# S5 feedthrough tables on four column tiles, and eleven front matmuls, in an S5/MoBA trunk

## The chip, the cores and the metric

The kernel runs on one core of a Trainium2 chip. The metric is the device time of one execution in microseconds (us). Three executions of the kernel before took 1000.97, 1001.4 and 1001.5 us; the median is 1001.4. In the text PE is TensorE, DVE is VectorE, ACT is ScalarE, POOL is GpSimd and SP is SyncE, which issues most of the transfers.

## What is computed

Two layers on a sequence of 256 tokens of width 1024, batch 1, all in float32. A layer is

```python
h = h + 0.5 * swiglu(rms_norm(h), w_gate, w_up, w_down)
h = h + mixer(rms_norm(h))         # layer 0: S5, layer 1: MoBA attention
h = h + 0.5 * swiglu(rms_norm(h), w_gate, w_up, w_down)
```

The feed-forward parts have an inner width of 2816. The change touches the S5 mixer, a diagonal state-space layer of 64 groups with 16 channels and 64 complex states each:

```python
u = h @ w_in
dt = exp(log_dt); lam = exp((a_re + i a_im) * dt)
coef = (lam - 1) / (a_re + i a_im);  bb = coef * b
state[t] = lam * state[t-1] + bb @ u[t]          # per group
y = Re(c @ state) + d * u
g = gelu(y); g = g * sigmoid(g @ w_glu); out = g @ w_out
```

## The kernel before

**Stages.** `phases` runs in order: f00 (first feed-forward part), S5, f01, f10, MoBA, f11. Every large product is a sum of three: activations and weights are each split into a high part that the matmul takes as float32r and a low remainder, and high x high, high x low and low x high are added (`mm3`, L396). Weights stream through three raw buffers of 1 MB (class `Stream`); `split` (L72) makes the high half on ACT (L84, L90) and the low half on DVE (L85, L91), and `pump` is called at fixed places in the product loops.

**The front.** `busy(7)` (L1376) gives PE seven products of ones; `quarter(0)` transposes the first quarter of x (L1332) into two PSUM tiles and writes the activations' high part on ACT (L1339) and low part on DVE (L1340); `busy(3)` follows; `gu0` (L457) then takes the first feed-forward column block by quarters of the depth (L471), and between its parts come quarters 1 to 3 of x. `quarter` uses the PSUM tiles `A1` and `A3`, of which there is one each, so a quarter's transposes have to wait until the quarter before has been read by L1339 and L1340. The sums of squares (L1354) go to POOL (`factors`, L1356), whose result goes through PE and DVE back to columns (L1365 to L1372).

**The tables.** S5 does not scan over all tokens; it works on pieces of four tokens, and a generator, `tables` (L618), prepares the matrices for that while f00 runs. `fill` (L1316) advances a slot counter by 0.7 or 1.4 at each step of the f00 products and calls the generator once per step; a `yield` hands control back. First come the parameters (L658 to L802): the exponentials on ACT, and sine, cosine, powers and `coef` as a long chain of small POOL instructions (helpers at L686, L690 and L692), with one reciprocal on DVE (L774). Then a loop (L919) runs a list of DVE work, each piece due at a slot and paid from a credit that grows with the slots, and PE work `later`, at slots set by `LAG` and `PACE`. The powers of lambda (`e_init`, `e_step`, L697 to L715) begin with a DVE copy of POOL's result (L701). For each of eight blocks `b` of four pairs of groups, `spread` (L844) lays the block-diagonal factors out, `t1_tab` (L856) transposes and stores the input table `dA`, and `t3_tab` (L872) makes the feedthrough table: the response of output token t to input token s inside a piece of four, with `d` on its diagonal. For a block it is

- eight products, one for each of four pairs and real and imaginary part, 32 rows by 64 columns each, all into PSUM partitions 0 to 31 (L880), and a ninth that adds the diagonal `DG[b]` with the identity (L882);
- eight ACT copies out of PSUM (L886), for each of four input tokens s and two groups g, to partitions 32 s to 32 s + 31, shifted by s and masked by `gm` so that a group does not reach its neighbour;
- one POOL send of 128 x 512 values to `dB[b]` (L888).

`d_diag` (L867) makes the diagonal on POOL. S5 loads `dA`, `dE` and `dB` back (L945 to L955). Its products use halves of the output partitions: L986 alternates between PSUM partitions 0 to 63 and 64 to 127.

```python
for i in range(2):                                              # t1, L982
    for q in range(4):
        c = i * 256 + q * 64
        for r in HALVES:
            mm(ps[r, c:c + 64], tv[:, i, q, r], U[:, 4 * b + q, :, :], start=True, stop=True)   # L986
```

Of the kernel before, what the change touches and what calls it, by code (L numbers as in the profile page):

```python
# [10 lines left out]
F32 = mybir.dt.float32  # L11
F32R = mybir.dt.float32r
AF = mybir.ActivationFunctionType
OP = mybir.AluOpType
AX = mybir.AxisListType
# [103 lines left out]
def trunk_kernel(ctx: ExitStack, tc, x, ffn_norm, ffn_w_gate, ffn_w_up, ffn_w_down, mix_norm,  # L119
# [3 lines left out]
    nc = tc.nc  # L123
# [13 lines left out]
    def psR():  # L137
        return pp.tile([128, 512], F32, name="pR", tag="R", bufs=2)
# [4 lines left out]
    mm = nc.tensor.matmul  # L143
# [6 lines left out]
    dB = [dp.tile([128, 1536], F32, name=f"dB_{b}") for b in range(NB)]  # L150
# [84 lines left out]
    ident = cst[:, 0:128]  # L235
# [7 lines left out]
    h = [h2[:, t, :] for t in range(2)]  # L243
# [22 lines left out]
    if "s5" in phases:  # L266
        rho = cp.tile([128, 32], F32, name="rho")
        tstack, lstack, xstack = ExitStack(), ExitStack(), ExitStack()
        tabp = tstack.enter_context(tc.tile_pool(name="tab", bufs=1))
        scn = tabp.tile([32, 2, 128], F32, name="scn")  # L270
        ldt = tabp.tile([32, 2], F32, name="ldt")
        dnat = tabp.tile([32, 32], F32, name="dnat")
        nc.gpsimd.dma_start(ldt, s5_log_dt[0].rearrange("(q g) -> q g", g=2))
        nc.gpsimd.dma_start(scn[:, 0, :], s5_a_re[0].rearrange("(q g) p -> q (g p)", g=2))
        nc.gpsimd.dma_start(scn[:, 1, :], s5_a_im[0].rearrange("(q g) p -> q (g p)", g=2))
        nc.gpsimd.dma_start(dnat, s5_d[0].rearrange("(q c) -> q c", c=32))
    st = Stream(nc, units, rp, hp)

    gT = cp.tile([128, 48], F32, name="gT")
# [17 lines left out]
    X = {}  # L297
# [320 lines left out]
    def tables(tp):  # L618

        V, P = nc.vector, nc.gpsimd  # L620

        def T(name, *shape):
            return tp.tile([128] + list(shape), F32, name=name)
# [9 lines left out]

        MPs = [T(f"mp{k}", 2, 4, 4, 2, 16) for k in range(2)]
        TT = T("tt", 2, 4, 4, 2, 16)
        t3s = [T(f"t3{k}", 4, 4, 32) for k in range(2)]
        cf7 = T("cf7", 7, 2)
        for k, n in enumerate(range(15, 1, -2)):
            for i in range(2):
                P.memset(cf7[:, k, i:i + 1], (-1.0) ** ((n - i) // 2) / math.factorial(n - i))  # L640
        for m in MPs + [TT] + t3s:
            P.memset(m, 0.0)
        bn = [tp.tile([128, 32, 16], F32, name="bn", tag="n0", bufs=2) for i in range(2)]
        cn = tp.tile([128, 1280], F32, name="cn", tag="n1", bufs=2)[:, 0:1024].rearrange("p (i a c) -> p i a c", i=2, c=64)
# [16 lines left out]
        ps = psR()  # L661
# [2 lines left out]
        nc.tensor.transpose(ps[:, 64:96], dtb.rearrange("q g p -> q (g p)"), ident[0:32, 0:32])  # L664
        prm = T("prm", 3, 32)
        V.tensor_copy(prm.rearrange("p a b -> p (a b)"), ps[:, 0:96])
        gm = tp.tile([32, 2], F32, name="gm")
        i2 = ident[0:32, 0:32].rearrange("p (g n) -> p g n", g=2)
        V.reduce_sum(gm, i2, axis=AX.X)
        i16 = tp.tile([32, 16], F32, name="i16")  # L670
        P.tensor_tensor(i16, i2[:, 0], i2[:, 1], op=OP.add)
        dTq = T("dTq", 32)
        ar, ai, dt = prm[:, 0, :], prm[:, 1, :], prm[:, 2, :]
        are, aim, mag = T("are", 32), T("aim", 32), T("mag", 32)
        tt(are, ar, dt, OP.mult)
# [3 lines left out]
        yield  # L679

        ps = psR()
        nc.tensor.transpose(ps[0:32, 0:32], dnat, ident[0:32, 0:32])
        V.tensor_copy(dTq[0:32, :], ps[0:32, 0:32])

        def pt(o, a, b, op):
            P.tensor_tensor(o, a, b, op=op)  # L686
# [1 line left out]
        def pts(o, a, s1, op0, s2=None, op1=None):  # L688
            if op1 is None:
                P.tensor_scalar(o, a, s1, None, op0=op0)  # L690
            else:
                P.tensor_scalar(o, a, s1, s2, op0=op0, op1=op1)  # L692
# [27 lines left out]
        q, y, y2, e0, e1, den = (T(n, 32) for n in ("q", "y", "y2", "e0", "e1", "den"))  # L720
# [50 lines left out]
            pt(lt[:, 1, :, o], u2[:, 1], w2[:, 0], OP.add)  # L771

        cfr, cfi = T("cfr", 32), T("cfi", 32)
        V.reciprocal(rden, den)  # L774
        pts(y, lr, -1.0, OP.add)
        pt(e0, y, ar, OP.mult)
# [15 lines left out]
        for i, a in enumerate((ltr, lti)):  # L792
            av = a.rearrange("p (b q) s -> p b q s", b=8)
            for k in range(2):
                P.tensor_copy(L[i][:, :, 0, k], av)
                for s in range(3):
                    o = L[i][:, :, 1, k, :, s]
# [46 lines left out]
        def spread(b):  # L844

            d_diag(b)
            tv, mv = (o.rearrange("p i q s g n -> p (i q) s g n") for o in (TT, MPs[b % 2]))
            zv = ZC[b].rearrange("p m i q (s n) -> p m (i q) s n", n=16)
            for g, r in enumerate(HALF):
                nc.scalar.activation(tv[r, :, :, g, :], zv[r, 0, :, 1:5], AF.Copy)  # L850
                nc.scalar.activation(mv[r, :, :, g, :], zv[r, 1, :, 1:5], AF.Copy)
            for i in range(2):
                nc.gpsimd.dma_start(dB[b][:, 512 * i:512 * i + 512].rearrange("p (q x) -> p q x", q=4),
                                    TT[:, i].rearrange("p q t g n -> p q (t g n)"))
# [10 lines left out]
        DG = {}  # L865

        def d_diag(b):  # L867
            DG[b] = tp.tile([32, 4, 16], F32, name="dg", bufs=2)
            P.tensor_tensor(DG[b], i16[:, None, :].to_broadcast([32, 4, 16]),
                            dTq[0:32, 4 * b:4 * b + 4, None].to_broadcast([32, 4, 16]), op=OP.mult)  # L870

        def t3_tab(b):  # L872

            t3 = t3s[b % 2]
            ps = psR()
            zc = ZC.pop(b)
            pk = ps[0:32, 0:256].rearrange("p (q t c) -> p q t c", q=4, c=16)
            for qq in range(4):
                for i in range(2):
                    mm(ps[0:32, qq * 64:(qq + 1) * 64], MPs[b % 2][:, i, qq, 3].rearrange("p g n -> p (g n)"),  # L880
                       zc[:, 0, i, qq, 0:64], start=qq == 0 and i == 0, stop=False, skip_group_check=True)
            mm(pk[:, :, 0, :], ident[0:32, 0:32], DG.pop(b), start=False, stop=True, skip_group_check=True)  # L882
            tv = t3.rearrange("p q t (g c) -> p q t g c", c=16)
            for s in range(4):
                for g in range(2):
                    nc.scalar.activation(tv[32 * s:32 * s + 32, :, s:4, g, :], pk[:, :, 0:4 - s, :], AF.Identity,  # L886
                                         scale=gm[:, g:g + 1])
            nc.gpsimd.dma_start(dB[b][:, 1024:1536], t3.rearrange("p q t c -> p (q t c)"))  # L888

        work = []  # L890

# [10 lines left out]
        def add_spread(b):  # L902
            work.append((0.0, B_AT, (spread, b), [(t3_tab, b), (t1_tab, b, 0), (t1_tab, b, 1)], 3 * (b - 1)))
# [15 lines left out]
        while work or later or dma:  # L919
# [4 lines left out]
            if later and later[0][0] <= now:  # L924
                f = later.pop(0)
                f[1](*f[2:])
                done[0] += 1
            while work and work[0][1] <= now and credit >= work[0][0] and done[0] >= work[0][4]:
                w, _, f, pe, _ = work.pop(0)
                f[0](*f[1:])  # L930
                credit -= w
                t = max([now + LAG] + [a[0] + PACE for a in later])
# [369 lines left out]

    pre = []
    tab = tables(tabp) if "s5" in phases else iter(())
    next(tab, None)
    slot = [0]
# [16 lines left out]
    def quarter(q, mid=lambda: None):  # L1323

        if not X:
            X[phases[0], "x"] = True
            X["h"], X["l"] = home(XP[0], phases[0])
        pv = [psA(1 + 2 * k)[:, 0:256] for k in range(2)]
        for k in range(2):
            for t in range(2):  # L1330
                c = (2 * q + k) * 128
                nc.tensor.transpose(pv[k][:, t * 128:(t + 1) * 128].rearrange("p (s i) -> p i s", s=4),  # L1332
                                    xn[t][:, c:c + 128], ident)
            if k == 0:
                mid()
        for k in range(2):
            g = gT[:, 2 * q + k:2 * q + k + 1]
            xh, xl = (X[p][:, 2 * q + k, :] for p in "hl")
            nc.scalar.activation(xh, pv[k], AF.Identity, scale=g)  # L1339
            nc.vector.scalar_tensor_tensor(xl, pv[k], g, xh.bitcast(F32), op0=OP.mult, op1=OP.subtract)  # L1340

    def busy(n):

        ps = psR()
        for _ in range(n):
            mm(ps[:, 0:128], ones, ones, start=True, stop=True)
# [29 lines left out]
    busy(7)  # L1376
    quarter(0, gains)
    busy(3)
    st.pump()
    next(tab, None)  # L1380
    square(0, 0)
# [68 lines left out]
```

## Time and profile before

| what | value |
|---|---|
| median of the runs shown | 1001.4 us |
| the profiled execution's own time | 1001.1 us |
| its span, first to last instruction | 999.3 us |
| granted PE clock, mean | 0.996 |
| busy: PE, DVE, ACT, POOL | 979.9, 703.3, 575.7, 167.2 us |
| transfers | 198.67 MB, mean 199 GB/s |

The profile is one execution. A line such as `50.41 0.39 PE L398 MATMUL pM<-wlo,xa 128*128 128x512 f32 x1` gives the start and the length in us, the engine, the source line, the operation, the tile written and those read, the size of the weights (128 rows by 128 columns), of the moving operand, and how many records are merged in the line. A matmul in plain float32 leaves two records, one for each pass. What stands in brackets at the end is the idle time before it and what ended that. The same stage can be asked for as a table by stretch, as groups by line, and as the chain of work that ended last.

### The profile page before, as it was taken

To read this page: it belongs to the slowest core of one execution; us is meant where nothing else is said; L and a number is where in the kernel's file an instruction comes from. 1 tells how busy PE (TensorE), PEld (TensorE's weight loads), DVE (VectorE), ACT (ScalarE), POOL (GpSimd) and SP (SyncE) were. 2 spreads that over 40 slices of the span, in tenths; PEclk is the share of its full clock that TensorE was granted. 3 is DMA by queue.
4 is the path that set the end of the run, shared out by engine and by line. 5 is a ranking of instruction groups with operands and counts; after the bars stand their busy time and mean duration, and the time that the engine had idled before them with its cause. 6 is when DMAs were issued, how large, how long until landed. Compare 5 with 4: busy or idle time off the path is not lost.

```text
span 999.3 us, 17186 instructions
## 1 busy us (share of the span) xinstructions
PE 979.9 (98%) x6700; PEld 870.9 (87%) x6700; DVE 703.3 (70%) x1147; ACT 575.7 (58%) x1045; POOL 167.2 (17%) x330
## 2 busy tenths in 40 slices
PE   8999999999889999999999999999999999999998
PEld 6778888888778999999999999998888899999997
DVE  4799676858978776666657766665689667766662
ACT  6647778744245655555455655553798656555541
POOL 4881222113740100000010000000441010000000
PEclk9999999999999999999999999999999999999999
DMA  8978776886846566555527665655354446756531
GB/s 234 275 259 257 263 250 214 277 325 217 283 139 214 179 199 219 184 192 185 189 81 227 215 209 175 206 172 171 128 169 148 154 162 212 241 180 210 170 128 42
DMA packets 138081, 198.67 MB, mean 199 GB/s; under 512 B 16320, under 2 KB 109584, under 8 KB 137744
## 3 DMA queue, kind: packets, MB, share of 16 engines
q1 hardware_dynamic: 133808, 184.32, 57.1%
q0 software_dynamic: 3616, 12.66, 3.2%
q8 instruction: 52, 0.85, 0.4%
q10 hardware_dynamic: 576, 0.61, 0.3%
q14 instruction: 29, 0.24, 0.1%
HBM read 183.89 MB, written 13.66 MB: 198 GB/s over the span
## 4 chain that ended last, share of the span: by engine, by line
PE 86%; DVE 7%; POOL 3%; issue 2%; ACT 2%; DMA 1%; SPq 0%; ACTq 0%; DVEq 0%
PE pM L552 12%; PE pM L551 12%; PE pM L553 12%; PE pA L397 9%; PE pA L399 9%; PE pA L398 9%; PE pM L397 5%; PE pM L398 5%; PE pM L399 5%; DVE wlo L85 2%; DVE zo L1011 1%; POOL sc L686 1%; PE pR L331 1%; PE pR L880 1%; ACT whi L84 1%
## 5 line engine op out<-in xcount | busy, mean ns | idle before, releaser
L551 PE MATMUL pM<-xa,whi 128*128 128x256 f32 x1056 | 295.7, 280 | 0.0
L552 PE MATMUL pM<-xa,whi 128*128 128x256 f32 x1056 | 294.9, 279 | 0.0
L553 PE MATMUL pM<-xa,wlo 128*128 128x256 f32 x1056 | 294.7, 279 | 0.0
L91 DVE SCALAR_TENSOR_TENSOR wlo<-raw,gT,whi 128x512 fp32r<-128x512 f32 x328 | 228.1, 747 | 71.2 <-ACT whi L90 71.0
L85 DVE TENSOR_TENSOR wlo<-raw,whi 128x1024 fp32r<-128x1024 f32 (+1 forms) x157 | 191.6, 1234 | 57.6 <-ACT whi L84 56.4
L90 ACT ACTIVATE whi<-raw,gT 128x512 fp32r<-128x512 f32 x328 | 213.6, 711 | 19.6 <-PE pA L399 14.7
L552 PEld LDWEIGHTS pM<-xa,whi 128*128 128x128 f32 x1056 | 198.5, 188 | 2.6
L551 PEld LDWEIGHTS pM<-xa,whi 128*128 128x128 f32 x1056 | 198.5, 188 | 2.3
L553 PEld LDWEIGHTS pM<-xa,wlo 128*128 128x128 f32 x1056 | 198.5, 188 | 0.0
L84 ACT ACTIVATE whi<-raw 128x1024 fp32r<-128x1024 f32 (+1 forms) x157 | 160.9, 1049 | 28.0 <-DMA raw<-in_ffn_w_up_dram 6.4
L397 PE MATMUL pA<-whi,ah 128*128 128x512 f32 x352 | 138.8, 394 | 0.0
L398 PE MATMUL pA<-wlo,ah 128*128 128x512 f32 x352 | 137.6, 391 | 0.0
L399 PE MATMUL pA<-whi,al 128*128 128x512 f32 x352 | 137.6, 391 | 0.0
L566 ACT ACTIVATE sg<-gr 128x256 f32<-128x256 f32 x66 | 27.6, 418 | 165.8 <-DVE gr L563 165.8
L397 PE MATMUL pM<-whi,xa 128*128 128x512 f32 x288 | 119.5, 415 | 0.0
L398 PE MATMUL pM<-wlo,xa 128*128 128x512 f32 x288 | 113.1, 393 | 1.1 <-DVE wlo L85 0.8
L399 PE MATMUL pM<-whi,xa 128*128 128x512 f32 x288 | 112.7, 391 | 0.0
L346 POOL TENSOR_TENSOR ms<-ss 128x1 f32<-128x1 f32 x10 | 1.9, 193 | 472.0 <-ACT sq L343 472.0
L399 PEld LDWEIGHTS pA<-whi,al 128*128 128x128 f32 x352 | 66.1, 188 | 14.4
L397 PEld LDWEIGHTS pA<-whi,ah 128*128 128x128 f32 x352 | 66.1, 188 | 11.5
L398 PEld LDWEIGHTS pA<-wlo,ah 128*128 128x128 f32 x352 | 66.2, 188 | 11.3
L563 DVE TENSOR_TENSOR gr<-pM,rrow 128x512 f32<-128x512 f32 x66 | 45.5, 689 | 40.6 <-PE pM L553 40.5
(262 smaller groups left out, 1234.9 us busy)
## 6 DMA issues: line engine op xcount, KB each, us to landing
raw<-in_ffn_w_down_dram SPq DMA_DIRECT2D x44, 1024.0 KB, 5.8
raw<-in_ffn_w_gate_dram SPq DMA_DIRECT2D x80, 512.0 KB, 4.0
raw<-in_ffn_w_up_dram SPq DMA_DIRECT2D x80, 512.0 KB, 5.1
raw<-in_moba_w_qkv_dram SPq DMA_DIRECT2D x12, 1024.0 KB, 5.2
TB<-dB SPq DMA_DIRECT2D x8, 768.0 KB, 6.1
raw<-in_ffn_w_gate_dram SPq DMA_DIRECT2D x16, 256.0 KB, 4.4
raw<-in_ffn_w_up_dram SPq DMA_DIRECT2D x16, 256.0 KB, 4.8
dB<-tt POOLq DMA_DIRECT2D x16, 256.0 KB, 5.3
```

The costliest lines, as they stand in the source:

```text
L84: nc.scalar.activation(hi[:, c], r[:, c], AF.Copy)
L85: nc.vector.tensor_tensor(lo[:, c], r[:, c], hi[:, c].bitcast(F32), op=OP.subtract)
L90: nc.scalar.activation(hi[:, c], r[:, c], AF.Identity, scale=g)
L91: nc.vector.scalar_tensor_tensor(lo[:, c], r[:, c], g, hi[:, c].bitcast(F32), op0=OP.mult, op1=OP.subtract)
L397: mm(o, xh, wh, start=start, stop=False)
L398: mm(o, xh, wl, start=False, stop=False)
L399: mm(o, xl, wh, start=False, stop=stop)
L551: mm(o, a, xh, start=k == 0 and i == 0, stop=False, skip_group_check=True)
L552: mm(o, a, xl, start=False, stop=False, skip_group_check=True)
L553: mm(o, b, xh, start=False, stop=k == 7, skip_group_check=True)
L563: V.tensor_tensor(gr, ps.rearrange("p (i c) -> p i c", i=2), Rr["row"][:, None, :].to_broadcast([128, 2, 256]), op=OP.mult)
L566: nc.scalar.activation(sg, gr[:, 0, :], AF.Silu)
```

## The change

`t3_tab` puts the four pairs on four column tiles: pair qq writes PSUM partitions 32 qq to 32 qq + 31, so eight products fill 128 partitions by 64 columns; the ninth product goes. Two ACT copies with the masks move this into a tile `kt` of seven steps in time, of which the first three stay zero. POOL adds the diagonal to step 3 in place, and four POOL sends write pieces of `kt`, each shifted by one step, to the rows of input token s in `dB[b]`. `d` is loaded as 8 x 128 and transposed to a column for each block; the identity is folded to `i32` (128 x 32) and the masks are made from it, for all 128 partitions. Five `yield`s move the reciprocal, and the POOL work behind it, five steps of `fill` later. In the order of DVE's instructions the reciprocal then stands behind the copy to `rr` (L1372) and before the split that follows it. At the front, eleven 128 x 256 products of the activations with themselves, whose result nobody reads, follow `busy(3)`; the first four read the high part, the last seven read the low part as well.

```diff
-        dnat = tabp.tile([32, 32], F32, name="dnat")
+        dnat = tabp.tile([8, 128], F32, name="dnat")
...
-        nc.gpsimd.dma_start(dnat, s5_d[0].rearrange("(q c) -> q c", c=32))
+        nc.gpsimd.dma_start(dnat, s5_d[0].rearrange("(b c) -> b c", c=128))
...
-        t3s = [T(f"t3{k}", 4, 4, 32) for k in range(2)]
+        kts = [T(f"kt{k}", 7, 2, 16) for k in range(2)]
...
-        for m in MPs + [TT] + t3s:
+        for m in MPs + [TT] + kts:
             P.memset(m, 0.0)
...
-        gm = tp.tile([32, 2], F32, name="gm")
-        i2 = ident[0:32, 0:32].rearrange("p (g n) -> p g n", g=2)
-        V.reduce_sum(gm, i2, axis=AX.X)
-        i16 = tp.tile([32, 16], F32, name="i16")
-        P.tensor_tensor(i16, i2[:, 0], i2[:, 1], op=OP.add)
-        dTq = T("dTq", 32)
+        i32 = T("i32", 2, 16)
+        V.reduce_sum(i32.rearrange("p g n -> p (g n)"), ident.rearrange("p (q x) -> p x q", q=4), axis=AX.X)
+        gm = T("gm", 2)
+        V.reduce_sum(gm, i32, axis=AX.X)
+        dT = T("dT", 8)
...
-        nc.tensor.transpose(ps[0:32, 0:32], dnat, ident[0:32, 0:32])
-        V.tensor_copy(dTq[0:32, :], ps[0:32, 0:32])
+        nc.tensor.transpose(ps[:, 0:8], dnat, ident[0:8, 0:8])
+        V.tensor_copy(dT, ps[:, 0:8])
...
         cfr, cfi = T("cfr", 32), T("cfi", 32)
+        for _ in range(5):
+            yield
         V.reciprocal(rden, den)
...
         def d_diag(b):
-            DG[b] = tp.tile([32, 4, 16], F32, name="dg", bufs=2)
-            P.tensor_tensor(DG[b], i16[:, None, :].to_broadcast([32, 4, 16]),
-                            dTq[0:32, 4 * b:4 * b + 4, None].to_broadcast([32, 4, 16]), op=OP.mult)
+            DG[b] = tp.tile([128, 2, 16], F32, name="dg", bufs=2)
+            P.tensor_scalar(DG[b], i32, dT[:, b:b + 1], None, op0=OP.mult)
...
-            t3 = t3s[b % 2]
+            kt = kts[b % 2]
             ps = psR()
             zc = ZC.pop(b)
-            pk = ps[0:32, 0:256].rearrange("p (q t c) -> p q t c", q=4, c=16)
-            for qq in range(4):
-                for i in range(2):
-                    mm(ps[0:32, qq * 64:(qq + 1) * 64], MPs[b % 2][:, i, qq, 3].rearrange("p g n -> p (g n)"),
-                       zc[:, 0, i, qq, 0:64], start=qq == 0 and i == 0, stop=False, skip_group_check=True)
-            mm(pk[:, :, 0, :], ident[0:32, 0:32], DG.pop(b), start=False, stop=True, skip_group_check=True)
-            tv = t3.rearrange("p q t (g c) -> p q t g c", c=16)
+            for i in range(2):
+                for qq in range(4):
+                    mm(ps[32 * qq:32 * qq + 32, 0:64], MPs[b % 2][:, i, qq, 3].rearrange("p g n -> p (g n)"),
+                       zc[:, 0, i, qq, 0:64], start=i == 0, stop=i == 1)
+            pk = ps[:, 0:64].rearrange("p (t c) -> p t c", c=16)
+            for g in range(2):
+                nc.scalar.activation(kt[:, 3:7, g, :], pk, AF.Identity, scale=gm[:, g:g + 1])
+            P.tensor_tensor(kt[:, 3], kt[:, 3], DG.pop(b), op=OP.add)
             for s in range(4):
-                for g in range(2):
-                    nc.scalar.activation(tv[32 * s:32 * s + 32, :, s:4, g, :], pk[:, :, 0:4 - s, :], AF.Identity,
-                                         scale=gm[:, g:g + 1])
-            nc.gpsimd.dma_start(dB[b][:, 1024:1536], t3.rearrange("p q t c -> p (q t c)"))
+                o = dB[b][32 * s:32 * s + 32, 1024:1536].rearrange("r (q x) -> q r x", q=4)
+                nc.gpsimd.dma_start(o, kt[:, 3 - s:7 - s].rearrange("p t g n -> p (t g n)"))
...
     busy(3)
+    ps = psR()
+    for a in ("h",) * 4 + ("l",) * 7:
+        mm(ps[:, 0:256], X[a][:, 1, 0:128], X["h"][:, 1, :], start=True, stop=True)
     st.pump()
```

## Prediction

> **What bounds the kernel now.** I read the page first, then the chain of work, then busy time by stretch, then the instructions around the changed lines in order of time.
>
> ```profile
> span 999.3 us, 17186 instructions
> PE 979.9 (98%) x6700; PEld 870.9 (87%) x6700; DVE 703.3 (70%) x1147; ACT 575.7 (58%) x1045; POOL 167.2 (17%) x330
> ...
> PE 86%; DVE 7%; POOL 3%; issue 2%; ACT 2%; DMA 1%; SPq 0%; ACTq 0%; DVEq 0%
> PE pM L552 12%; PE pM L551 12%; PE pM L553 12%; PE pA L397 9%; PE pA L399 9%; PE pA L398 9%; PE pM L397 5%; PE pM L398 5%; PE pM L399 5%; DVE wlo L85 2%; DVE zo L1011 1%; POOL sc L686 1%; PE pR L331 1%; PE pR L880 1%; ACT whi L84 1%
> ```
>
> TensorE (PE) is busy 98% of the span and is 86% of the chain that ends last. The line that the change rewrites, L880, stands on that chain by itself with 1%. In the two stretches below the fields are length, then busy time (and count) of PE, weight loads, DVE, ACT, POOL, then granted clock, DMA share, GB/s:
>
> ```profile
> 68.00:96.00 28.00, 27.55 (x124) 22.54 (x124) 26.27 (x36) 17.45 (x25) 6.36 (x13) 1.00 0.81 257
> 96.20:207.00 110.80, 110.80 (x625) 89.97 (x624) 77.49 (x112) 83.53 (x159) 26.22 (x49) 1.00 0.77 264
> ```
>
> All eight L880 groups lie in the second stretch (first and last start below). There PE is busy 110.80 of 110.80 us at full clock; DVE has 30% to spare, ACT 25%, POOL 76%, DMA 23%. Nothing else is late next, so PE time saved there is saved from the end.
>
> **The change, part by part.**
>
> *The t3 products (L880, L882).* One group in order of time (start, duration; a duration includes the pipeline, so I count from start to start):
>
> ```profile
> 96.00 0.40 PE L399 MATMUL pM<-whi,xa 128*128 128x512 f32 x1
> 96.33 1.08 PE L880 MATMUL pR<-zc,mp 128*32 128x64 f32 x16
> 97.34 0.29 PE L882 MATMUL pR<-dg,cst 32*32 32x64 f32 x2
> 97.56 0.50 PE L397 MATMUL pM<-whi,xa 128*128 128x512 f32 x1
> 97.90 0.40 PE L398 MATMUL pM<-wlo,xa 128*128 128x512 f32 x1
> 98.13 0.40 PE L399 MATMUL pM<-whi,xa 128*128 128x512 f32 x1
> ```
> ```profile
> L880 PE MATMUL pR<-zc,mp x128: 219/219/243, 96.3 to 197.9; 128*32 128x64 f32 x128
> ```
>
> From L399 at 96.00 to L398 at 97.90 are 1.90 us. Without the group two steps would lie there; one is L398 to L399 at the end of the fence, 0.23, so 0.46 in all. The group costs 1.90 - 0.46 = 1.44 us, and 128 records at 16 a group are 8 groups: 11.5 us of PE. A product leaves two records (fp32 takes two passes). The new code drops L882 and puts the same eight products on four column tiles of 32, one after another. No four-tile matmul is in this trace; the nearest is L986, which alternates between two column tiles of 64:
>
> ```profile
> 237.43 0.39 PE L399 MATMUL pM<-whi,xa 128*128 128x512 f32 x1
> 237.74 1.15 PE L986 MATMUL pA<-U,TA 128*64 128x64 f32 x32
> 238.82 0.50 PE L397 MATMUL pM<-whi,xa 128*128 128x512 f32 x1
> 239.16 0.40 PE L398 MATMUL pM<-wlo,xa 128*128 128x512 f32 x1
> ```
>
> Its 32 records cost 239.16 - 237.43 - 0.46 = 1.27 us, less than today's 18. Short slices show how, first a group's first records and then those still running near its end:
>
> ```profile
> 96.33 0.24 PE L880 MATMUL pR<-zc,mp 128*32 128x64 f32 x1
> ```
> ```profile
> 237.74 0.28 PE L986 MATMUL pA<-U,TA 128*64 128x64 f32 x2
> ```
> ```profile
> 97.02 0.39 PE L880 MATMUL pR<-zc,mp 128*32 128x64 f32 x4
> ```
> ```profile
> 238.49 0.40 PE L986 MATMUL pA<-U,TA 128*64 128x64 f32 x8
> ```
>
> L880 begins with one record; its last four start from 97.02, so 12 took 0.69 us: 0.058 each. L986 begins with two at once, though the program emits both passes of a product before the other tile's; its last eight start from 238.49, so 24 took 0.75 us: 0.031 each, 0.062 for a pair. So a tile works its own records off in turn, and the tiles run beside each other. With four tiles each has four records. Entering and leaving cost L986 1.27 - 15 x 0.062 = 0.34; plus three steps, 3 x 0.062 = 0.19, is 0.53; 0.02 more for two further tiles to start gives 0.55 us for a group. I take that: 1.44 - 0.55 = 0.89 saved, times 8 is **7.1 us**. Ends: two tiles' rate, 15 x 0.031 + 0.34 = 0.81, saves 0.63 x 8 = 5.0; no overlap at all saves only L882, 97.34 to 97.56, 0.22 x 8 = 1.8; at best the group costs entering and leaving plus three of L880's steps, 0.34 + 0.17 = 0.51, saving 7.4.
>
> The Trainium skill speaks against this: TensorE: Matmul & The Clock Gate, Part 3 (the mechanism of packing), says that a weight load overlaps running matmuls only when its row group differs. Column tiles share all rows, so by that rule the sum would be the 1.8 us of no overlap. L986's tiles share all rows too and start in pairs at 0.031 us a record, so the trace disagrees; the same page's table gives three column tiles a measured 2.38x, which no run here shows.
>
> *Copies, diagonal and sends.*
>
> ```profile
> 96.20:207.00 110.80, 21.08 (x64) 1.00 0.77 264
> ```
> ```profile
> L886 ACT ACTIVATE t<-pR,gm 32x64 f32<-32x64 f32 x16 | 4.0, 296 | 0.1
> ...
> L888 POOL DMA_DIRECT2D dB<-t x8 | 4.3, 539 | 28.5 <-ACT t L886 28.5
> ...
> L869 POOL TENSOR_TENSOR dg<-i,dTq 32x64 f32<-32x64 f32 x6 | 2.0, 338 | 0.1
> ```
>
> L886 takes ACT 21.08 us (first row, that line alone), 2.6 a group. Two copies of 64 elements a partition (0.296 each) replace eight: ACT gains 2.0 us a group, worth nothing to the end, since PE waits for ACT nowhere there. POOL: one send of 0.539 becomes four, and an in-place add is new (0.34 as L869, perhaps 1.3 beside DVE): 2 to 3 us a group, at most 24 us on an engine that is free for 84. The add waits for ACT, and behind it on POOL stand the sends, the next pair's zc copy and the dA sends. But the old send waited for ACT as well, 28.5 us in sum, and that wait ends 2 us earlier as ACT has less to copy. So nothing behind it moves by more than about 1 us; its readers (the next group some 14 us on, and S5's loads after the last group) do not see it. Cost 0; if POOL came later than a group's 14 us, PE would wait.
>
> *Front matmuls.* Eleven 128x256 products stand between the warm-up matmuls and L471:
>
> ```profile
> 5.26 0.83 PE L1346 MATMUL pR<-ones 128*128 128x128 f32 x6
> ```
> ```profile
> 5.82 0.87 DVE L1340 SCALAR_TENSOR_TENSOR xa<-pA,gT,xa 128x256 fp32r<-128x256 f32 x2 [0.54 <-ACT xa L1339]
> ```
> ```profile
> 7.97 0.80 PE L471 MATMUL pA<-whi,xa 128*128 128x512 f32 x1 [1.88 <-ACT whi L84]
> ```
> ```profile
> 4.56:7.97 3.41, 1.53 (x11) 1.18 (x10) 1.08 (x4) 1.52 (x4) 3.35 (x6) 1.00 0.96 303
> 7.97:11.38 3.41, 3.41 (x9) 2.17 (x9) 2.03 (x3) 2.34 (x5) 0.00 (x0) 0.50 1.05 352
> ...
> 284.42:287.83 3.41, 2.11 (x51) 1.88 (x52) 2.25 (x5) 1.88 (x4) 2.69 (x3) 1.00 0.51 207
> 287.83:291.25 3.42, 3.42 (x39) 3.25 (x40) 2.25 (x5) 2.22 (x4) 2.14 (x2) 1.00 0.00 0
> ```
>
> PE idles 1.88 us before 7.97. The first four can start near 6.1, the last seven at 6.69 when DVE's second row is written; at half of a 512-column step (0.23), 0.115 each, they end at 6.69 + 0.80 = 7.5, inside the idle time. At half clock they would end near 8.6: 0.6 us lost. What they change is the clock: after a stretch with 1.53 us of PE work the next runs at 0.50; after one with 2.11 it runs at 1.00. With 1.53 + 1.27 = 2.8 us I expect 1.00 from 7.97, and PE ready for the next transposes about 1.3 us sooner. But:
>
> ```profile
> 10.62 1.22 DVE L85 TENSOR_TENSOR wlo<-raw,whi 128x1024 fp32r<-128x1024 f32 x1 [1.38 <-ACT whi L84]
> ...
> 12.36 0.88 DVE L1340 SCALAR_TENSOR_TENSOR xa<-pA,gT,xa 128x256 fp32r<-128x256 f32 x2
> ```
> ```profile
> 13.25 0.60 PE L1332 MATMUL pA<-cst,xn 128*128 128x128 f32 x4
> ```
>
> DVE's L85 follows ACT and a transfer, not PE, and ends at 11.84; the parameter copy, now two reductions, and L1340 follow, to 13.24 or a little later. The transposes of quarter 2 (L1332, 13.25) write the two PSUM tiles that L1340 reads, of which there is one each, so they stay near 13.2. I take 0.2 us gained, with ends at 0.6 lost and 1.3 gained.
>
> *The later reciprocal.*
>
> ```profile
> 19.33 0.62 POOL L1357 TENSOR_TENSOR ms<-ss 128x2 f32<-128x2 f32 x1 [11.37 <-ACT sq L1354]
> ```
> ```profile
> 23.89 0.35 DVE L774 RECIPROCAL rden<-den 128x32 f32<-128x32 f32 x1 [2.35 <-POOL den L686]
> ...
> 46.02 0.23 DVE L701 COPY e<-c 128x16 f32<-128x16 f32 x1 [3.86 <-POOL c L692]
> ```
> ```profile
> 25.38 0.50 PE L398 MATMUL pM<-wlo,xa 128*128 128x512 f32 x1 [0.81 <-DVE wlo L85]
> ...
> 53.05 0.44 PE L495 MATMUL pR<-cst,act 128*128 128x128 f32 x2 [1.33 <-DVE act L482]
> ```
>
> DVE's wait of 2.35 us and PE's of 0.81 behind it go. POOL's sine chain, which starts behind 19.33 and hands c to DVE at 46.02, has the same work beside the same DVE splits. DVE comes to L701 earlier and waits longer; PE's 1.33 at L495 becomes about 2.1. Late next is POOL, and the 0.81 is given back: 0.1 gained, between 0.7 lost (the split that moves forward lands on POOL's root) and 0.8 gained.
>
> **Sum.** The profiled execution took 1001.1 us (span 999.3 and 1.8 around it): 1001.1 - 7.1 - 0.3 = 993.7. The median of the runs, 1001.4, stands 0.3 above it, so **994.0 us**.
>
> **Rivals** (all with that 0.3). **A, records held in order:** PE starts a tile's second pass only after its first and holds the next tile behind it; two tiles' rate, 5.0 saved: 996.4 less the front's 0.3, 996.1. The pair at 237.74 speaks against it. **B, no overlap** on 32-wide tiles: 1.8 saved, 999.3. Against it: L986. **C, the front pays:** POOL's chain shortens as DVE leaves it alone, and the 1.3 and 0.8 us both reach the end: 1001.4 - 7.1 - 2.1 = 992.2. For it: the chain runs through POOL there; against it: the transfer before 10.62 and the wait at 46.02. **D, slower:** each change of column tile empties the array. In today's group the last L880 starts at 97.02 + 3 x 0.058 = 97.19 and L882, of another tile shape, at 97.34: 0.09 over a step. At seven changes a group costs 0.34 + 15 x 0.058 + 7 x 0.09 = 1.84, that is 0.40 x 8 = 3.2 more than now: 1004.3. It decides from 0.03 us a change. Against it: L986 changes tile at nearly every record at 0.031. The Trainium skill, TensorEngine Tiling (Array Packing), Key Properties, says that only a change of tiling mode drains; L986 agrees.
>
> **How the numbers follow.** Forecast 0.64, A 0.13, B 0.05, C 0.13, D 0.05. The likeliest case alone spans 993 to 995. Leaving out B, D and the outer part of C, the range is 991.5 to 997.0. Faster by over 0.2% (about 2 us, what a measurement can tell from no change) is below 999.4: forecast, A, C and half of B, 0.92. Within it: the other half of B, and D where a change costs little, 0.04. Slower: the rest of D, 0.04.
>
> **What would show it.** Right: the new product line as 16 records whose first four start within 0.03 us, about 0.55 us of PE a group and no L882; granted clock 1.00 from 7.97 to 11.38, yet L1332 of quarter 2 still near 13.2; no DVE wait at the reciprocal and a longer one at L701. Wrong: steps of 0.03 or 0.058 with single starts (A, B), gaps at each tile (D), quarter 2 near 12 or c near 44 (C), or PE waits between 96 and 207 that are not there now.

## The result, and the profile after

Five executions of the kernel after took 992.96 to 995.05 us, median 993.93; five of the kernel before on the same chip 1000.59 to 1001.5, median 1000.97. The ratio is 0.9927 (95% interval 0.9916 to 0.9938). The forecast was 994.0 us, in a range of 991.5 to 997.0.

The page of the kernel after, its span, the engines' busy time and the chain of work by engine and by line:

```profile
span 991.9 us, 17175 instructions
...
PE 973.8 (98%) x6695; PEld 866.0 (87%) x6695; DVE 703.3 (71%) x1148; ACT 559.2 (56%) x997; POOL 192.1 (19%) x361
...
PE 84%; DVE 7%; POOL 3%; issue 2%; ACT 2%; DMA 1%; SPq 0%; ACTq 0%; DVEq 0%; POOLq 0%
PE pM L551 12%; PE pM L552 12%; PE pM L553 12%; PE pA L397 9%; PE pA L399 9%; PE pA L398 9%; PE pM L397 5%; PE pM L398 5%; PE pM L399 5%; DVE wlo L85 2%; DVE zo L1010 1%; POOL sc L685 1%; PE pR L331 1%; ACT whi L84 1%; PE pR L861 1%
```

The span is 7.4 us shorter. The products of `t3_tab` (L880 before, L879 now) are gone from the chain's lines. POOL is busy 25 us longer, ACT 16.5 us shorter.

The first group of these products in order of time, the kernel after:

```profile
95.55 0.40 PE L399 MATMUL pM<-whi,xa 128*128 128x512 f32 x1
95.87 0.43 PE L879 MATMUL pR<-zc,mp 128*32 128x64 f32 x16
96.23 0.50 PE L397 MATMUL pM<-whi,xa 128*128 128x512 f32 x1
96.58 0.39 PE L398 MATMUL pM<-wlo,xa 128*128 128x512 f32 x1
```

L399 to L398 are 1.03 us; less two steps, 0.46, the group costs 0.57 us, where it cost 1.44. Done so for each of the eight groups, the sums are 11.39 us before and 4.40 after: 6.99 saved. (One of the eight follows L495 and not L399, in both kernels; what that adds to a sum cancels in the difference.) Short slices show how the records of this group start (the first from 95.86 to 95.90, the second from 95.86 to 95.97):

```profile
95.87 0.26 PE L879 MATMUL pR<-zc,mp 128*32 128x64 f32 x4
```
```profile
95.87 0.31 PE L879 MATMUL pR<-zc,mp 128*32 128x64 f32 x7
```

Four records have started within 0.03 us; 0.10 us after the first, seven have. By the trace's starts the sixteen come in four rounds of four, 0.08, 0.06 and 0.06 us apart. The trace does not name a record's column tile. That a round holds one record of each tile is inferred: there are four tiles, and 0.06 us is also the step of one tile alone in the kernel before.

From 96 to 201 us (length, then busy time and count of PE, weight loads, DVE, ACT, POOL, then granted clock, DMA share, GB/s) nothing took the place of what went:

```profile
96.00:201.00 105.00, 105.00 (x613) 84.77 (x610) 77.51 (x112) 68.25 (x113) 50.31 (x83) 1.00 0.83 276
```

The same stretch for ACT's copies (L883), for POOL's add (L884) and for its sends (L887) alone:

```profile
96.00:201.00 105.00, 4.09 (x16) 1.00 0.83 276
```
```profile
96.00:201.00 105.00, 5.56 (x8) 1.00 0.83 276
```
```profile
96.00:201.00 105.00, 22.51 (x32) 1.00 0.83 276
```

Sixteen copies take 4.09 us, where sixty-four took 21.08. POOL's add is 0.70 us each and its sends 0.70 each, 28.07 in all for 4.3 before, 3.0 us more a group, on an engine that is busy 50 of 105 us. PE does not wait once.

The front, PE in order of time:

```profile
5.42 1.49 PE L1345 MATMUL pR<-ones 128*128 128x128 f32 x6
6.56 1.69 PE L1380 MATMUL pR<-xa 128*128 128x256 f32 x11
8.08 1.25 PE L471 MATMUL pA<-whi,xa 128*128 128x512 f32 x4
...
11.44 0.61 PE L471 MATMUL pA<-wlo,xa 128*128 128x512 f32 x2
13.22 0.83 PE L1331 MATMUL pA<-cst,xn 128*128 128x128 f32 x4 [1.16 <-DVE xa L1339]
```

The waits of PE, first before and then after (line waited for, us in total, times, longest):

```profile
PE pA L471 <- ACT whi L84: 1.9, 1, 1.9
PE pR L495 <- DVE act L482: 1.3, 1, 1.3
...
PE pM L398 <- DVE wlo L85: 0.8, 1, 0.8
```
```profile
PE pR L495 <- DVE act L482: 1.7, 2, 1.4
PE pA L1331 <- DVE xa L1339: 1.2, 1, 1.2
```

The eleven products fill the wait at L471. The transposes of quarter 2 start at 13.22, where they started at 13.25, after a new wait of 1.16 us. L398's wait is gone, the one at L495 is 0.4 us longer in sum.

### The profile page after: what moved, and what is told of

Its sections match the earlier page's. It is cut to its first block, busy times and chain, and to the rows that moved or that the text cites. A ratio compares the mean times of both kernels' runs of the same rounds, so it can differ in the third digit from the quotient of the medians.

```text
span 991.9 us, 17175 instructions
## 1 busy us (share of the span) xinstructions
PE 973.8 (98%) x6695; PEld 866.0 (87%) x6695; DVE 703.3 (71%) x1148; ACT 559.2 (56%) x997; POOL 192.1 (19%) x361
## 4 chain that ended last, share of the span: by engine, by line
PE 84%; DVE 7%; POOL 3%; issue 2%; ACT 2%; DMA 1%; SPq 0%; ACTq 0%; DVEq 0%; POOLq 0%
PE pM L551 12%; PE pM L552 12%; PE pM L553 12%; PE pA L397 9%; PE pA L399 9%; PE pA L398 9%; PE pM L397 5%; PE pM L398 5%; PE pM L399 5%; DVE wlo L85 2%; DVE zo L1010 1%; POOL sc L685 1%; PE pR L331 1%; ACT whi L84 1%; PE pR L861 1%
## 5 line engine op out<-in xcount | busy, mean ns | idle before, releaser
L85 DVE TENSOR_TENSOR wlo<-raw,whi 128x1024 fp32r<-128x1024 f32 (+1 forms) x157 | 191.4, 1234 | 55.6 <-ACT whi L84 54.7
L398 PE MATMUL pA<-wlo,ah 128*128 128x512 f32 x352 | 137.6, 391 | 0.0
L399 PE MATMUL pA<-whi,al 128*128 128x512 f32 x352 | 137.6, 391 | 0.0
L398 PE MATMUL pM<-wlo,xa 128*128 128x512 f32 x288 | 113.1, 393 | 0.1
L399 PE MATMUL pM<-whi,xa 128*128 128x512 f32 x288 | 112.7, 391 | 0.0
L399 PEld LDWEIGHTS pA<-whi,al 128*128 128x128 f32 x352 | 66.1, 188 | 14.3
L398 PEld LDWEIGHTS pA<-wlo,ah 128*128 128x128 f32 x352 | 66.2, 188 | 11.3
L563 DVE TENSOR_TENSOR gr<-pM,rrow 128x512 f32<-128x512 f32 x66 | 45.5, 689 | 40.9 <-PE pM L553 40.8
```

Of the source, the lines that this page charges most:

```text
L85: nc.vector.tensor_tensor(lo[:, c], r[:, c], hi[:, c].bitcast(F32), op=OP.subtract)
L398: mm(o, xh, wl, start=False, stop=False)
L399: mm(o, xl, wh, start=False, stop=stop)
L563: V.tensor_tensor(gr, ps.rearrange("p (i c) -> p i c", i=2), Rr["row"][:, None, :].to_broadcast([128, 2, 256]), op=OP.mult)
```

## Experiments

Ratios are to the kernel before on the same chip, with 95% intervals. "Groups" is the PE cost of all eight, worked out as above from each trace.

| run | median us | ratio | groups us |
|---|---|---|---|
| after | 993.93 | 0.9927 (0.9916 to 0.9938) | 4.40 |
| e1, tables alone | 994.28 | 0.9936 (0.9923 to 0.9948) | 4.40 |
| e2, front matmuls alone | 1000.91 | 1.0003 (0.9994 to 1.0012) | 11.4 |
| e3, yields alone | 1000.08 | 0.9993 (0.9984 to 1.0002) | 11.4 |
| e4, before without the ninth product | 999.08 | 0.998 (0.9971 to 0.9989) | 9.61 |
| e5, pair as the outer loop | 994.06 | 0.993 (0.9916 to 0.9943) | 4.55 |
| e6, products doubled | 995.5 | 0.9942 (0.9929 to 0.9956) | 6.20 |
| e7, own PSUM for quarter 2 | 993.27 | 0.992 (0.9908 to 0.9933) | 4.40 |
| e8, POOL's chain earlier | 991.81 | 0.9905 (0.989 to 0.992) | 4.40 |
| e9, e7 and e8 together | 991.87 | 0.9908 (0.9894 to 0.9921) | 4.40 |
| e10, e9 without front matmuls | 991.83 | 0.9911 (0.9897 to 0.9924) | 4.40 |
| e11, e9 without yields | 991.84 | 0.9908 (0.9895 to 0.9922) | 4.40 |
| e12, e9 with B's loads later | 992.6 | 0.9922 (0.9908 to 0.9936) | 4.40 |

**Which part pays: e1, e2, e3.** e1 is the kernel after without these lines:

```diff
-        for _ in range(5):
-            yield
...
-    ps = psR()
-    for a in ("h",) * 4 + ("l",) * 7:
-        mm(ps[:, 0:256], X[a][:, 1, 0:128], X["h"][:, 1, :], start=True, stop=True)
```

e2 is the kernel before with the last three of them added, e3 with the first two.

> The change's table part alone, without the eleven front matmuls and without the five yields. My theory (all of the gain is the overlap of the t3 products on four column tiles; front and yields give some 0.3 us): eight groups at 0.55 us of TensorE instead of 1.42, so 7.0 us faster than before, 994.0, within 0.5 us of the changed kernel. Rival (front matmuls and the later reciprocal pay 1.3 and 0.8 us that reach the end): 2 us slower than the changed kernel, about 996.

> The kernel before with the eleven front matmuls alone. My theory: granted clock 1.00 where the kernel before could run at 0.50 behind 8 us, TensorE early at the transposes of quarter 2, but these wait for VectorE's read of the one pair of PSUM tiles; 0 to 0.3 us gained, 1000.8. Rival (the warm clock is worth its 1.3 us): 999.7. Other rival: at half clock they end late and cost 0.6 us, 1001.6.

> The kernel before with the five yields ahead of the reciprocal alone. My theory: VectorE's 2.35 us wait at the reciprocal and TensorE's 0.81 us go, VectorE's wait for GpSimd's result at L701 grows from 3.9 to about 5 us and TensorE's wait for act behind it from 1.3 to about 2; 1000.9, no change. Rival (the 0.81 us reaches the end): 1000.2.

The tables alone give all of the gain that can be told apart from none; neither of the other two parts alone moves the time by more than its interval. In e2 the wait at L471 is gone and a wait of 0.5 us at L1332 is new, the exchange that was expected. e3 came out otherwise. Its 1000.08 us is the rival's 1000.2 rather than the expected 1000.9, though its interval still holds no change. PE's wait of 0.8 us at L398 is gone, but DVE's wait for POOL's `c` is 2.97 us, where it was 3.86 and was to grow to 5; PE's waits at L495 are 1.7 us in sum, the longest 1.2, where there was one of 1.3. So the later reciprocal does more than move a wait; the section on the prediction says what.

**How much is the ninth product: e4.** The kernel before, whose table then lacks `d`:

```diff
-                       zc[:, 0, i, qq, 0:64], start=qq == 0 and i == 0, stop=False, skip_group_check=True)
-            mm(pk[:, :, 0, :], ident[0:32, 0:32], DG.pop(b), start=False, stop=True, skip_group_check=True)
+                       zc[:, 0, i, qq, 0:64], start=qq == 0 and i == 0, stop=qq == 3 and i == 1, skip_group_check=True)
+            DG.pop(b)
```

> The kernel before without the ninth product (L882) of each group: the diagonal term with d is left out of the feedthrough table. It splits the gain: my theory gives the ninth product its steps from L880's end to the next product, 0.22 us, so 8 x 0.22 = 1.8 us faster, 999.2, with each group at 1.2 us of TensorE. The rest of the 7 us (5.2) is then the overlap of the tiles. Rival (the ninth product's change of tile shape is the main cost of a group): 4 us or more faster, 997 or less.

Its first group in order of time:

```profile
97.19 0.40 PE L399 MATMUL pM<-whi,xa 128*128 128x512 f32 x1
97.52 1.08 PE L880 MATMUL pR<-zc,mp 128*32 128x64 f32 x16
98.53 0.50 PE L397 MATMUL pM<-whi,xa 128*128 128x512 f32 x1
98.87 0.40 PE L398 MATMUL pM<-wlo,xa 128*128 128x512 f32 x1
```

The group costs 1.68 - 0.46 = 1.22 us, 0.22 less. Over the eight it is 11.39 - 9.61 = 1.78 us. The other 9.61 - 4.40 = 5.2 us are the overlap of the four tiles: sixteen records of the same size on one tile span 1.08 us, on four tiles 0.43.

**How the tiles take their records: e5, e6.** e5 swaps the two loops (`qq` outside, `i` inside), so that both products of a tile, four records, come before the next tile's. e6 computes each product twice (`for i in (0, 1, 0, 1)`).

> The changed kernel with the products in the order of the kernel before: for each pair both products one after another, so that a column tile gets its four records in a row before the next tile gets any. Theory of a queue for each tile, deep enough: the tiles still run beside each other, group about 0.55 us, 994. Theory that the overlap comes from the order (a tile holds the next tile's records back once it has two waiting): a tile's four records take 4 x 0.058 us before the next begins or half of that, group 0.8 to 1.3 us, 2 to 6 us slower than the changed kernel, 996 to 1000.

> The changed kernel with each group's eight products made twice (same result, the second time written over the first). Theory of four tiles side by side: four more records for each tile, 4 x 0.058 = 0.23 us a group, 8 x 0.23 = 1.9 us slower than the changed kernel, 995.8. If the records were handed out in turn at two tiles' rate: 16 x 0.031 = 0.5 a group, 4 us slower, 998. One after another: 16 x 0.058 x 8 = 7.4 us slower, 1001.3.

First groups of e5 and of e6:

```profile
95.51 0.40 PE L399 MATMUL pM<-whi,xa 128*128 128x512 f32 x1
95.83 0.45 PE L879 MATMUL pR<-zc,mp 128*32 128x64 f32 x16
96.22 0.50 PE L397 MATMUL pM<-whi,xa 128*128 128x512 f32 x1
96.55 0.39 PE L398 MATMUL pM<-wlo,xa 128*128 128x512 f32 x1
```
```profile
95.05 0.40 PE L399 MATMUL pM<-whi,xa 128*128 128x512 f32 x1
95.37 0.65 PE L879 MATMUL pR<-zc,mp 128*32 128x64 f32 x32
95.96 0.50 PE L397 MATMUL pM<-whi,xa 128*128 128x512 f32 x1
96.30 0.40 PE L398 MATMUL pM<-wlo,xa 128*128 128x512 f32 x1
```

e5: 1.04 - 0.46 = 0.58 us, so the order matters by 0.01 to 0.02 us a group. Its records start in rounds of four as well, the first four within 0.04 us and the fifth 0.08 us after the first. With all four records of a tile given out in a row, the next tiles' first records must then have passed three that were still waiting (again read from the rounds, as the trace names no tile). e6: 1.25 - 0.46 = 0.79 us. Sixteen more records, four more rounds, cost 0.22 us more, 0.056 a round, and the time of 995.5 us is near the 995.8 expected for four tiles side by side, not the 998 or 1001.3 of the other two cases. A group of after is then three such steps behind the first round, 0.17 us, and about 0.38 for the first round and for entering and leaving.

**What holds the front: e7, e8.** e7 is the kernel after with a PSUM tile of its own for quarter 2; e8 is the kernel after with the front of POOL's chain one slot ahead of the B loads and the rest one `yield` later.

```diff
-        pv = [psA(1 + 2 * k)[:, 0:256] for k in range(2)]
+        pv = [(psM() if q == 2 else psA(1 + 2 * k))[:, 0:256] for k in range(2)]
```
```diff
         pt(y2, y, y, OP.mult)
+        yield
...
-             (1, 1): pre,
+             (1, 1): [lambda: next(tab, None)] + pre,
```

> The changed kernel with quarter 2 of x transposed into two other PSUM tiles, so that its transposes no longer wait for VectorE's read of quarter 1. Theory: TensorE's wait of 1.2 us there goes, but GpSimd's sine chain starts only some tenths earlier and hands its result to VectorE near 45 us; TensorE waits for act as much longer near 52 us; 0 to 0.5 us faster than the changed kernel, 993.7. Rival (the front is bound by that wait): 1.2 us faster, 992.7.

> The changed kernel with the first half of GpSimd's sine chain (to y squared) ahead of the factors of the norm on its queue, where it idles until 19.5 us. Theory (between 20 and 68 us the end hangs on GpSimd's chain): its result comes 3 to 5 us earlier, VectorE's wait at L701 goes or nearly so, TensorE's 1.4 us wait for act near 52 us goes, 1 to 2 us faster than the changed kernel, 992.4. Rival (GpSimd's chain is covered by something else that is late, VectorE's splits): no change, 993.9.

In e7 the wait at L1331 is gone, but L495 waits 2.2 us; 993.27 lies between the two expectations and cannot be told from 993.93. In e8 every execution (991.59 to 992.06) is below the fastest of the kernel after (992.96) and of e5 to e7 (992.66). POOL's `den` and DVE's copy of `c` in e8, from the two engines in order of time:

```profile
12.71 0.25 POOL L685 TENSOR_TENSOR den<-e,e 128x32 f32<-128x32 f32 x1
```
```profile
42.39 0.19 DVE L700 COPY e<-c 128x16 f32<-128x16 f32 x1
```

`den` comes 11.5 us earlier than in the kernel after (24.22), and DVE's copy has no wait ahead of it, where it had one of 3.85. The other traces say the same. In the nine without this change (before, after, e1 to e7) DVE's copy of `c` starts anywhere from 44.64 to 47.22 us, and the L399 ahead of the first group follows it each time by 49.95 to 50.02 us. In e8 that L399 starts at 93.82, 1.7 us earlier than after, and 51.4 behind the copy. So POOL's chain did hold the end, and about 2 us of it could be had (2.1 by the medians): this version beats both kernels.

**What is late next: e9 to e12.** e9 joins e7 and e8. e10 and e11 are e9 without the eleven front matmuls and without the five yields (the lines of e1's diff). e12 is e9 with the eight loads of B taken out of the front and put at later slots:

```diff
-    extra = [(30.0, more_loads), (50.0, more_gains)] + [(54.0 + 6 * s, lambda s=s: ld_h(s)) for s in range(4)]
+    extra = sorted([(30.0, more_loads), (50.0, more_gains)] + [(54.0 + 6 * s, lambda s=s: ld_h(s)) for s in range(4)]
+                   + [(34.0 + 2 * s, p) for s, p in enumerate(pre)], key=lambda e: e[0])
...
-             (1, 1): [lambda: next(tab, None)] + pre,
+             (1, 1): [lambda: next(tab, None)],
```

> The kernel after with both changes of the two runs before this: GpSimd's table work begins one step earlier, and the front matmuls write a PSUM tile of their own. Theory (quarter 2's transposes wait 1.0 us for VectorE only because of the shared PSUM tile, and with GpSimd early nothing behind them swallows the gain): that wait goes and the time is 991.0 us, 0.8 below the run with GpSimd early alone. Rival (the factors of the norm from GpSimd are late next and swallow it): 991.8, with a longer wait of TensorE for them.

> As e9_early_own, without the eleven matmuls of nothing at the front. Theory (they pay only by holding the granted clock at full rate behind them, and what GpSimd's late table work swallowed before is free now): where the clock's records show half rate in 7 to 11 us the front is some 1 us longer, the time 992.0; where they show full rate, no difference. Rival (the front is set by VectorE and GpSimd whatever the clock): within 0.2 us of e9_early_own.

> As e9_early_own, without the five yields that put VectorE's reciprocal of the table behind the front. Theory (the reciprocal's input comes early when GpSimd begins early, so VectorE no longer stands in its queue for it): within 0.3 us of e9_early_own. Rival (the reciprocal still blocks VectorE's queue ahead of the front's copies): 0.8 us or more slower, with VectorE waiting at the reciprocal's line.

e9 came out at its rival's time, but not by the rival's mechanism. Its chain of waits from 5 to 45 us, and PE at L495 behind it:

```profile
10.02 0.59 PE pA L1332 x4
...
25.78 7.42 DMA raw<-in_ffn_w_up_dram
...
34.02 0.49 DVE act L482
34.56 0.44 PE pR L495 x2
```
```profile
34.56 0.44 PE L495 MATMUL pR<-cst,act 128*128 128x128 f32 x2 [1.67 <-DVE act L482]
```

A transfer of 7.42 us, then a split, then DVE's L482: PE waits 1.67 us for it. The wait for the norm's factors, which the rival named, is 0.37. Now e10: the clock by stretch, its chain, and PE at L495.

```profile
5.11:8.52 3.41, 1.75 (x10) 1.24 (x11) 1.81 (x5) 2.25 (x6) 2.13 (x4) 1.00 1.05 342
8.52:11.93 3.41, 3.41 (x13) 2.40 (x12) 2.10 (x4) 1.77 (x4) 0.07 (x1) 0.50 1.05 362
```
```profile
11.11 1.00 PE pA L1332 x4
```
```profile
33.95 0.44 PE L495 MATMUL pR<-cst,act 128*128 128x128 f32 x2
```

Without the front matmuls 1.75 us of work were followed by a stretch at 0.50 clock, and quarter 1's transposes began 1.09 us later than in e9 (11.11 against 10.02). PE then did not wait at L495 at all, and got there no later (33.95 against 34.56). The time is e9's, 991.83 against 991.87, as e10's rival said. So in these two executions the front matmuls win PE about a microsecond at the clock, and it is spent waiting for a transfer. e11's expectation held: 991.84 against 991.87.

> The kernel of e9_early_own with the eight loads of B (64-byte pieces, sent by SyncE between 12.6 and 23.3 us, during which the transfers run at 67 GB/s from 20 to 25) moved some 25 us later, behind the up-projection's weight transfer that e9_early_own's chain of waits shows ahead of TensorE's 1.7 us wait at L495. Theory (those pieces hold that transfer up, and it swallowed what TensorE had gained ahead of it): the transfer lands before TensorE needs it, most of the 1.7 us wait goes, the time is 990.2 to 990.8 us. Rival (the transfers are full in any case, or GpSimd's and VectorE's table work is late next): the wait comes back at a later weight split, 991.8 us.

e12 was meant to let that transfer land earlier. The wait at 34 us is gone. But the last loads of B, sent until 63.1 us, came late for DVE, and then for PE; DVE and PE of e12 in order of time:

```profile
67.23 0.69 DVE L626 TENSOR_TENSOR z<-bn,cfr 128x512 f32<-128x512 f32 x1 [4.04 <-issue]
70.12 0.69 DVE L626 TENSOR_TENSOR z<-bn,ncf 128x512 f32<-128x512 f32 x1 [2.19 <-DMA bn<-in_s_b_im_dram]
```
```profile
78.62 0.44 PE L495 MATMUL pR<-cst,act 128*128 128x128 f32 x2 [0.88 <-DVE act L482]
```

DVE stood for 6.23 us, of which the profile gives 2.19 to a load of B and 4.04 to no releaser, and PE lost 0.88 here and 0.59 at 62 us (L822, for DVE's L498), where e9 lost nothing. 992.6 us with an interval that overlaps e9's decides nothing for the theory: the wait moved, as the rival said, though to a stop that the experiment itself had made. Whether a middle place for these loads would pay is open.

## Why the prediction was right, point by point

**Four tiles run beside each other: right.** The step was 1.44 - 0.55 = 0.89 a group, 7.1 in all. Measured: 0.55 a group on the mean (4.40 / 8; 0.55 to 0.57 in the seven that follow L399), 6.99 in all. It has two parts, told apart by e4: 1.78 us for L882 (the forecast's 1.8 for no overlap at all) and 5.2 for the overlap. The parts of the 0.55 were less exact: a round is 0.056 instead of 0.062 (e6), entering and leaving with the first round about 0.38 instead of 0.36, two small errors that cancel. The one place in the trace of before that showed two column tiles, L986, carried the whole forecast; what made it safe was counting its starts and not its busy time.

**PE time saved there is saved from the end: right.** 6.99 from the groups, and the first group's preceding L399 starts at 95.55 instead of 96.00: 0.45 from all that lies ahead. The sum is 7.44, the span's difference 7.4. From that L399 to the end are 903.33 us before and 896.32 after, 7.0 less, so nothing was given back behind. The 0.45 cannot be given to the change: without front matmuls and yields that L399 starts at 95.82 in e1 and at 97.19 in e4. The close agreement of 994.0 with 993.93 is in part luck. The forecast counts from 1001.4, the median of three executions; over five it is 1000.97, so 7.4 us were forecast and 7.04 measured, which the groups explain by themselves.

**Copies and sends at nothing: right.** POOL's 3.0 us more a group lies at the upper end of the 2 to 3 expected, and no wait of PE came with it.

**Front matmuls: the wait right, the clock not shown, and worth nothing that can be measured.** PE came 1.16 us early to quarter 2 (1.3 expected) and waited for L1339, which is L1340 of the kernel before, until 13.22 (near 13.2 expected). The wait is the shared PSUM pair, since it goes when the tile is another one (e7). One thing differed: in this execution `busy(3)` took 1.49 us instead of 0.83, and the eleven products ended at 8.25 instead of 7.5, so L471 began 0.11 us later than before and gained only afterwards. That comes from where full clock begins: its first record stands at 6.89 us here and at 4.56 before, and the products of ones start 0.21 us apart ahead of it here, and 0.11 apart behind it before. So the forecast's stretches, 4.56 to 7.97 and 7.97 to 11.38, are not those of this execution, and it does not show that the eleven products kept the clock up: e3 has full clock there without them. The start of POOL's chain (L1357, now L1356) gained nothing, 19.54 instead of 19.33.

**The later reciprocal: its own wait goes, the rest of the step failed.** The prediction said that DVE's wait of 2.35 us would turn up at L701 and that PE's wait at L495 would be 2.1. DVE and POOL after, and POOL before:

```profile
24.11 0.28 DVE L1366 COPY rT<-pR 2x128 f32<-2x128 f32 x1 [1.24 <-PE pR L1364]
...
25.72 0.34 DVE L775 RECIPROCAL rden<-den 128x32 f32<-128x32 f32 x1
```
```profile
45.56 0.23 DVE L700 COPY e<-c 128x16 f32<-128x16 f32 x1 [3.85 <-POOL c L691]
```
```profile
24.22 1.42 POOL L685 TENSOR_TENSOR den<-e,e 128x32 f32<-128x32 f32 x1
...
27.30 0.32 POOL L689 TENSOR_SCALAR q<-q 128x32 f32<-128x32 f32 x1
```
```profile
23.61 0.25 POOL L686 TENSOR_TENSOR den<-e,e 128x32 f32<-128x32 f32 x1
...
25.48 2.52 POOL L690 TENSOR_SCALAR q<-q 128x32 f32<-128x32 f32 x1
```

The reciprocal has no wait, as forecast. But 1.24 of the 2.35 us is now a wait at the copy to `rT`, which comes from POOL through PE, and L700 waits 3.85 us as it did before (3.86). PE's single wait at L495 is 1.4. DVE's copy of `c` comes 0.46 us earlier, and the first group with it, as in the nine traces told of under e8. The step that failed is that POOL's chain has the same work beside the same DVE splits. While DVE no longer stands still, its splits run beside `den` (0.25 us before, 1.42 after) and no longer beside the second `q` (2.52 before, 0.32 after). POOL loses 1.17 us there and 0.40 at L305, and gets back 2.2: from the start of L1357 (L1356 after) to the end of `c` are 25.99 us instead of 26.66. In the other kernels it is 26.4 to 26.7 us without the yields (e1, e2, e4) and 25.8 to 26.5 with them (e3, e5, e6, e7). So the 0.1 was too small in this trace, and that front and reciprocal together give 0.46, near the 0.3 of the forecast, is luck: it is 0.67 from the shorter chain, less the 0.21 by which that chain starts later. By the medians neither part can be told from nothing.

**The rivals.** A (5.0 saved, records in order): against it are four starts within 0.03 us and e5, where by the rounds the next tile's records pass three waiting ones. B (1.8 saved): e4 measures what B leaves, 999.08 us, and the kernel after is 5 us below it. The Trainium skill's rule behind B (TensorE: Matmul & The Clock Gate, Part 3), that a weight load overlaps only with matmuls of another row group, does not hold here: these tiles share all rows, their sixteen weight loads of 0.11 us each pass in 0.27 us, and the sixteen records in 0.43. D (a drain at each change of tile): by e5's and e6's rounds of 0.056 us for four tiles there is no room for it. C (the front pays, 992.2) did not come about, with 993.93 us and `c` at 45.5 instead of near 44. A part of its mechanism did, as POOL's chain is 0.67 us shorter. That more can be had on this chain is shown by e8 (991.81), through another change. The forecast saw that POOL's chain is late next; it did not ask whether it could start sooner.

## What to carry to other kernels

Small products that write 32 PSUM partitions each can share the array: put them on four column tiles, and sixteen float32 records of 64 columns take 0.43 to 0.45 us instead of 1.08, in either loop order. Price it by start-to-start times around the group, with entering, leaving and the first round counted (about 0.4 us here), for the length of a line overlaps the start of the next. A gain on an engine that then meets a wait is only lent: follow it to the next wait, and the next, before it goes into the sum; here 1.1 us of PE ended at a PSUM tile, then at POOL's chain, then at a weight transfer. What holds a stage shows best as a distance that stays the same over many executions, as the 50.0 us from `c` to the first group do; a few tenths of a microsecond in one profile prove nothing.

## What the runs showed of the hardware beyond what was expected

- Records of one tile that wait do not hold back those of the next: with all four records of a tile emitted before the next tile's (e5), four start within 0.04 us and the group costs 0.58 us instead of 0.57, so at least three stand waiting aside.
- The granted clock fell to 0.50 after stretches of 3.41 us with 1.53 us (before) and 1.75 us (e10) of PE work, and not after 2.11 us (before, 284.42). The amount of work alone does not decide it: stretches with 1.62 us (after, from 276.55) and 1.75 us (e9, from 31.56) were followed by full clock. Whether the front meets such a stretch depends on where the stretches fall, and full clock began anywhere from 3.92 to 9.47 us. Of the five profiled executions without the front matmuls the four in which it began by 5.11 fell back after that first stretch (before, e1, e4, e10), and e3, from 5.67, did not. Of the nine with them none fell back, but in only two did it begin as early (e5 at 4.42, e9 at 4.26; 3.10 and 3.17 us of work in that stretch). The Trainium skill (TensorE: Matmul & The Clock Gate, Part 1) gives an idle window as the condition; here a window half filled with work was enough in some places and not in others.
- A POOL instruction on 128 x 32 values (`den`) takes 0.25 us by itself and 1.42 us while DVE works at a split (L85), so moving DVE's work moves POOL's durations. Not all DVE work does this: beside L1340 in e8 `den` takes 0.25 us.
- Eight loads in pieces of 64 bytes can slow the transfers of a whole stretch: e9 from 20 to 25 us moved 67 GB/s, e12, without them there, 328 (the two lines below). Spread from 48.4 to 63.1 us in e12 they left 195 to 325 GB/s between 50 and 65, so it is not their size alone.

```profile
20.00:25.00 5.00, 4.63 (x22) 3.26 (x21) 3.62 (x6) 3.95 (x6) 4.44 (x9) 1.00 0.70 67
```
```profile
20.00:25.00 5.00, 4.69 (x22) 3.31 (x21) 3.63 (x7) 3.96 (x6) 4.36 (x10) 1.00 0.98 328
```
